# The first half step's output product as seven products of blocks, taken row tile by row tile

## The chip, the cores and the metric

The kernel runs on one core of a Trainium2 chip. The metric is the device time of one execution in microseconds (us). Engines are called as the profile calls them: PE (TensorE, matmul), PEld (its weight loads), DVE (VectorE), ACT (ScalarE), POOL (GpSimd) and SP (SyncE, which issues the DMA transfers).

## The reference

One layer of a diffusion backbone over 1024 latent tokens and 256 context tokens, 1024 features, all in float32. The part that matters here is the first half step and the norm after it:

```python
def swiglu(h, w_in, w_out):
    a, b = jnp.split(h @ w_in, 2, axis=-1)
    return (jax.nn.silu(a) * b) @ w_out
...
    x = x + 0.5 * ml[2] * swiglu(modulate(rms_norm(x, norm1_g), ml[0], ml[1]), ffn1_w_in, ffn1_w_out)
    hx = modulate(rms_norm(x, norm2_g), ml[3], ml[4])
    ... = jnp.split(hx @ w_in, SPLITS, axis=-1)        # token mixers, then a second half step
```

`ffn1_w_out` has 2816 rows (hidden features) and 1024 columns. The modulations `ml` are products of `silu(c)` with `w_mod`.

## The kernel before

Activations lie with the features in partitions: a feature tile is 128 partitions by 512 tokens. The 1024 latents are two chunks, `C0` and `C1`, of 512 tokens. Every matmul operand is split into two parts of fewer bits, `hi` and `lo` (`split`: a cast on ACT, then a subtraction `src - hi` on DVE), and a product is three matmuls: hi x hi, hi x lo, lo x hi.

A scheduler orders each engine's instructions ahead of time; all of a kernel's instructions carry the line number of one helper in the profile, so groups are told apart by the names of the tiles. Tiles come from pools with a fixed number of buffers: `raw` (loaded weights, 3), `wh` and `wl` (split operands, 4 each), a pool of 38 tiles of 4 KB a partition, a pool of 11 smaller ones, and PSUM with 5 banks for products (`ps`), 2 for transposes (`pt`) and 1 more (`po`).

The input products of both half steps and of the token mixers are made by the class `Winograd`: seven products of 2 x 2 blocks instead of eight. Its left operands are column tiles of the weights, summed on POOL (tiles `s`), its right operands (tiles `r`) sums of blocks of the normalised activations. The hidden features of the first half step are stored to a DRAM tensor `hd`, the latents to `xd`.

The output product of the first half step is made in the plain way. For each chunk, all 22 hidden tiles are loaded from `hd` and split (tiles `hid`); then, for groups of three, three and two feature tiles `d`, PE goes through the 22 hidden tiles in three blocks of 8, 8 and 6, with weights loaded and split by `load_w` (tiles `wh`, `wl`). Each `d` has one PSUM bank. When a group is done, DVE adds `gate * ps` to `x` and the result is stored to `xd`:

```python
for ch in (C0, C1):
    ...
    for ds in ((0, 1, 2), (3, 4, 5), (6, 7)):
        ps = {d: ps_s() for d in ds}
        for j0, j1 in ((0, 8), (8, 16), (16, NH)):
            for d in ds:
                wh, wl = load_w(...)
                for j in range(j0, j1):
                    matmul(ps[d], w, hs[j][:, 0], ...)
                    matmul(ps[d], w, hs[j][:, 1], ...)
                    matmul(ps[d], v, hs[j][:, 0], ...)
```

Other work is traced between these products. `steps` are the remaining modulations (`later_mod`: tiles `rawm` are loaded, multiplied by a column of `silu(c)` and added into `macc` on DVE). While the products of `C1` run, the second norm of `C0` is made (`norm0`: squares, a sum over partitions on PE, a reciprocal root, a broadcast by transposes, then the scaled tiles and their splits). `square` sums the squares of `C1` as its feature tiles become ready. After the stage `mix.start` makes ten products of `C0` (the first two of five pairs) while `norm1` makes the right operands of `C1`, whose scaled tiles are `h`, their differences `nt`.

Of the kernel before, what the change touches and what calls it, by code (L numbers as in the profile page):

```python
# [18 lines left out]
P = 128  # L19
D = 1024  # L20
# [29 lines left out]
def tile_dit_layer(  # L50
# [29 lines left out]
    class Engine:  # L80
        """An engine whose instructions stay in the order of the trace while strict[0] is set."""
# [72 lines left out]
    # Vectors over features become columns: one row of 128 each, transposed on the chip.  # L154
# [71 lines left out]
    def rsqrt_cols(a, n):  # L226
        """a ** -0.5 for a [P, n] > 0."""
# [12 lines left out]
    def rstd_cols(accs, n, dim):  # L240
        """(sum over accs and partitions + dim * eps) ** -0.5, tokens in partitions: [P, n / P]."""
# [12 lines left out]
    def bcast(y, n):  # L254
        """Columns y over tokens in partitions, as rows in all partitions: PSUM [P, n]."""
# [5 lines left out]
    def later_mod(m, halves=(0, 1), streams=None):  # L261
        """Columns of modulation m for the latents (0) and, where it is used, the context (1), in steps."""
# [54 lines left out]
    def first_mod(m, half, raws):  # L317
        """Half of modulation m of both streams, on the tensor engine alone; in steps: 6 tiles, 2, the columns."""
# [15 lines left out]
    def second_mod(m, half, raws):  # L334
        """The same of the latents alone; in steps: the products of each tile, their parts, their sums, the columns."""
# [23 lines left out]
    def norm_gain(name, m, gname):  # L359
        """g * (1 + scale) * sqrt(D) by stream; the shift is modulation m."""  # L360
# [59 lines left out]
    def modulated_norm(xs, hh, hl, ch, gain, mod, m):  # L420
        """In steps, for other work to be traced between: squares, sums, two halves of the rest."""
# [20 lines left out]
    def run(steps, n=None):  # L442
        """The next n steps (all without n)."""
# [7 lines left out]
    def out_pieces(w, js, spare=False):  # L451
        """Rows of w_out of hidden tiles js, by halves of the columns."""
# [10 lines left out]
    class Winograd:  # L463
        """Products with normalised latents by Winograd's seven products of 2 x 2 blocks.

        Blocks of the weights: two tiles of columns (a, b) by halves of the input features; blocks of
        the activations: halves of the features by halves of the tokens (C0, C1).
        """

        def __init__(self, xs, gain, mod, m, pairs, plain=False, ahead=3, side_from=None):  # L470
            """pairs: columns of each a and b; plain: with all parts of the latents themselves.

            ahead pairs are begun while the second tokens are normalised. side_from: from this pair on
            the plain left operands are given to side(i, operand) too, as 1, 2 (of a), 0, 4 (of b); those of
            the pairs before come after them.
            """
# [3 lines left out]
            self.n_ahead, self.side, self.started, self.n_left = ahead, None, [], 0  # L480
            self.source, self.ready = self.lefts(pairs, side_from), []

        def keep(self, i, k, src, lo_eng=None):
            """Feature tile k of right operand i."""
# [14 lines left out]
        def norm0(self, in_place=False):  # L499
            """In steps: squares, sums, two halves of the rest."""  # L500
# [13 lines left out]
        def square(self, d):  # L514
            """Feature tile d of the second tokens, squared, into the sums."""
            if d == 0:
                self.acc = [ttile("sq_acc")]
            sq = self.acc[0] if d == 0 else ttile("sq")
            act.activation(out=sq, in_=self.xs(d, C1), func=AF.Square)
            if d == KD - 1:  # L520
                self.acc.append(sq)
            elif d:
                dve.tensor_add(out=self.acc[0], in0=self.acc[0], in1=sq)

# [35 lines left out]
        def part_second(self, k):  # L560
            """The parts of tile k of the second tokens, in the place of the values."""
# [5 lines left out]
        def parts(self, k, ch):  # L567
            """Feature tile k of the latents, its two parts."""
# [3 lines left out]
        def lefts(self, pairs, side_from):  # L572
            """Left operands, in the order they are used."""
# [73 lines left out]
        def first(self):  # L647
            """The products with the first tokens alone: what the rest needs, and a of these tokens."""
# [5 lines left out]
        def start(self, norm):  # L654
            """The first products of some pairs, while the second tokens are normalised."""
# [17 lines left out]
        def start_together(self):  # L673
            """The same in steps: P1 of pairs 0, 1; of 2, 3; of each other; then the second products likewise."""
# [33 lines left out]
        def fetch(self):  # L708
            """What was begun of the next pair and put aside."""
# [14 lines left out]
        def second(self, u):  # L724
            """b of the first tokens."""
# [8 lines left out]
        def third(self, u, v):  # L734
            """a and b of the second tokens."""
# [65 lines left out]
    def turn_tokens(ch, toks, engines=("dve", "act")):  # L801
        """In steps of one feature tile."""
# [26 lines left out]
    def squares(ch, turn):  # L829
        """Squares of the feature tiles as they are turned, added up."""  # L830
# [105 lines left out]
    # Input products of the first half step, and the whole of it for the context.  # L936
# [33 lines left out]
    def context_out(j):  # L970
        """Output products of hidden tiles j - 1 and j for the context."""
# [46 lines left out]
    # Output products for the latents, all hidden tiles of 512 tokens at a time; the second norm starts  # L1018
    # while those of the second tokens are made.
# [9 lines left out]
    for ch in (C0, C1):  # L1029
        o = ch[1]  # L1030
        hs = []
        for j in range(NH):
            hs.append(load_parts("hid", hd[j, :, o : o + 512]))
        for k in range(KD):
            sp.dma_start(out=xs(k, ch), in_=xd[k, :, o : o + 512])
        n_done = 0
        for ds in ((0, 1, 2), (3, 4, 5), (6, 7)):
            ps = {d: ps_s() for d in ds}
            for j0, j1 in ((0, 8), (8, 16), (16, NH)):
                for d in ds:  # L1040
                    wh, wl = load_w(
                        ffn1_w_out[0][j0 * P : j1 * P, d * P : (d + 1) * P].rearrange("(k p) n -> p k n", p=P),
                        (j1 - j0, P),
                    )
                    for j in range(j0, j1):
                        w, v = wh[:, j - j0], wl[:, j - j0]
                        matmul(ps[d], w, hs[j][:, 0], start=j == 0, stop=False)
                        matmul(ps[d], w, hs[j][:, 1], start=False, stop=False)
                        matmul(ps[d], v, hs[j][:, 0], start=False, stop=j == NH - 1)
                    n_done += 1  # L1050
                    if ch == C0:
                        run(steps, 4)
                    elif n_done == 1:
                        run(steps)
                        gain2.update(norm_gain("gain2", 3, "g2"))
                        mix.gain = gain2["l"]
                    elif n_done in (2, 4, 6, 8):
                        run(norms2, 1)
            for d in ds:
                dve.scalar_tensor_tensor(  # L1060
                    out=xs(d, ch), in0=ps[d], scalar=gate1["l"][:, d : d + 1], in1=xs(d, ch),
                    op0=ALU.mult, op1=ALU.add,
                )
                sp.dma_start(out=xd[d, :, o : o + 512], in_=xs(d, ch))
# [4 lines left out]
    # Gated short convolution, and the gates.  # L1069
# [459 lines left out]
```

## Time and profile before

| | |
|---|---|
| median of three runs | 2813.86 us (2812.37 to 2816.64) |
| span of the profiled execution | 2813.7 us |
| busy: PE, PEld, DVE, ACT, POOL | 97%, 81%, 70%, 39%, 19% |
| share of the chain that ended last, by engine | PE 83%, DVE 9%, DMA 3% |

The profiled execution is told by its span, from the first to the last instruction; its time is within 0.2 us of the median of the runs. A busy share is a mean over stages with different limits, so a change in one stage is read in a stretch of the timeline. In a group of instructions, the name before `<-` is the tile written and those after it are the tiles read; what stands after the bar is the busy time, the mean duration of one in ns, the idle time before them and what ended it. In a timeline, an entry has its start, its time in us, its engine and the tiles; `x12` stands for twelve in a row.

### The profile page before, as it was taken

How to read it: one execution, taken by the hardware profiler on the slowest of the kernel's cores; microseconds unless marked ns; L12 is line 12 of the kernel's file. 1: busy time of each engine (PE TensorE's matmuls, PEld its weight loads, DVE VectorE, ACT ScalarE, POOL GpSimd, SP SyncE). 2: the span in 40 equal slices, each digit the busy share in tenths (PEclk: the TensorE clock that was granted, in tenths of full speed). 3: DMA queues.
4: the chain of work that ended last, by engine and by line, in shares of the span. 5: the costliest groups of instructions: out<-in, count | busy, mean ns of one | idle time of the engine just before them, and what ended most of it. 6: DMA issues, size and time to landing. Idle time of an engine off the chain costs nothing.

```text
span 2813.7 us, 37012 instructions
## 1 busy us (share of the span) xinstructions
PE 2725.5 (97%) x13741; PEld 2286.0 (81%) x13741; DVE 1957.2 (70%) x3218; ACT 1096.5 (39%) x2176; POOL 542.3 (19%) x433
## 2 busy tenths in 40 slices
PE   7898999999999989999999999999998999999998
PEld 4687988888888868888999888887886788888887
DVE  5886688877864387676568377776458766666667
ACT  3524333333433243333345167764245222232225
POOL 2541122121001054323123000000014221212111
PEclk8899999999999989999999999999999999999999
DMA  8264433445974333323313300002532311221111
GB/s 303 97 199 151 145 111 126 130 142 158 309 236 130 104 119 106 105 69 97 105 46 122 111 23 5 12 1 90 170 93 90 111 41 51 60 60 53 46 53 68
DMA packets 346910, 298.77 MB, mean 106 GB/s; under 512 B 25430, under 2 KB 276456, under 8 KB 346728
## 3 DMA queue, kind: packets, MB, share of 16 engines
q1 hardware_dynamic: 346728, 296.40, 32.9%
q8 instruction: 108, 1.77, 0.3%
q14 instruction: 74, 0.61, 0.1%
HBM read 247.54 MB, written 48.76 MB: 105 GB/s over the span
## 4 chain that ended last, share of the span: by engine, by line
PE 83%; DVE 9%; DMA 3%; issue 2%; ACT 2%; SPq 0%; POOL 0%; ACTq 0%; DVEq 0%; POOLq 0%
PE ps L88 73%; PE po L88 6%; PE pt L88 4%; DVE wl L88 2%; DVE r L88 1%; DVE nt L88 1%; DVE macc L88 1%; DMA raw<-in_ffn_w_out_dram 1%; DMA rawm<-in_w_mod_dram 1%; DVE wo L88 1%; DMA hid<-hd 1%; DVE h L88 1%; DVE uc L88 0%; SPq L88 0%; DMA mcol<-mrow 0%
## 5 line engine op out<-in xcount | busy, mean ns | idle before, releaser
L88 PE MATMUL ps<-r,wl 128*128 128x512 f32 x5280 | 1242.0, 394 | 36.9 <-ACT wl L88 12.8
L88 PEld LDWEIGHTS ps<-r,wl 128*128 128x128 f32 x5280 | 995.5, 190 | 256.1 <-ACT wl L88 16.4
L88 ACT CAST wl<-s 128x512 fp32r<-128x512 f32 x256 | 158.6, 620 | 330.3 <-PE ps L88 274.5
L88 ACT CAST wl<-raw 128x512 fp32r<-128x512 f32 x230 | 142.3, 620 | 245.7 <-PE ps L88 165.8
L88 DVE TENSOR_TENSOR wl<-raw,wl 128x512 fp32r<-128x512 f32 x228 | 167.1, 733 | 99.9 <-ACT wl L88 98.8
L88 DVE TENSOR_TENSOR wl<-s,wl 128x512 fp32r<-128x512 f32 x256 | 217.4, 850 | 11.6 <-ACT wl L88 9.8
L88 POOL TENSOR_TENSOR s<-raw,s 128x512 f32<-128x512 f32 x64 | 99.1, 1549 | 624.2 <-DVE wl L88 618.9
L88 PE MATMUL ps<-hid,wh 128*128 128x512 f32 x704 | 217.2, 390 | 1.4 <-ACT wh L88 1.4
L88 ACT CAST wh<-raw 128x1024 fp32r<-128x1024 f32 (+2 forms) x100 | 97.9, 982 | 251.5 <-PE ps L88 208.6
L88 DVE SCALAR_TENSOR_TENSOR x<-ps,gate_l,x 128x512 f32<-128x512 f32 (+1 forms) x200 | 140.7, 726 | 79.1 <-PE ps L88 78.8
L88 POOL TENSOR_TENSOR sq_acc<-sq_acc,sq 128x512 f32<-128x512 f32 (+1 forms) x33 | 41.8, 1268 | 765.4 <-ACT sq L88 764.6
L88 POOL TENSOR_TENSOR s<-raw 128x512 f32<-128x512 f32 x64 | 91.2, 1424 | 399.4 <-DMA raw<-in_ffn_w_in_dram 164.5
L88 DVE TENSOR_TENSOR wl<-raw,wh 128x1024 fp32r<-128x1024 f32 (+1 forms) x92 | 109.6, 1192 | 67.5 <-ACT wh L88 65.8
L88 PEld LDWEIGHTS ps<-hid,wh 128*128 128x128 f32 x704 | 131.7, 188 | 30.2 <-ACT wh L88 2.6
L88 DVE SCALAR_TENSOR_TENSOR macc<-rawm,silu_c,macc 128x512 f32<-128x512 f32 x168 | 141.4, 859 | 12.0 <-DMA rawm<-in_w_mod_dram 11.0
L88 PE MATMUL ps<-hid,wo 128*128 128x512 f32 (+1 forms) x552 | 147.7, 381 | 0.4 <-DVE x L88 0.3
L88 DVE TENSOR_TENSOR u<-u,ps 128x512 f32<-128x512 f32 x168 | 114.3, 680 | 46.6 <-PE ps L88 46.3
L88 PE MATMUL ps<-wh,r 128*128 128x256 f32 x768 | 141.5, 285 | 0.0
L88 PE MATMUL ps<-gh,wo 128*128 128x512 f32 (+1 forms) x368 | 135.5, 380 | 1.5 <-ACT wo L88 1.5
L88 PE MATMUL ps<-hid,wl 128*128 128x512 f32 x352 | 136.5, 389 | 0.0
L88 DVE TENSOR_REDUCE m<-ps 128x1 f32<-128x512 f32 (+1 forms) x192 | 112.7, 595 | 20.9 <-PE ps L88 19.8
L88 DVE TENSOR_TENSOR pts<-pt,pts 128x512 fp32r<-128x512 f32 x160 | 108.7, 683 | 18.8 <-ACT pts L88 18.4
(259 smaller groups left out, 4897.1 us busy)
## 6 DMA issues: line engine op xcount, KB each, us to landing
raw<-in_ffn_w_in_dram SPq DMA_DIRECT2D x114, 512.0 KB, 3.7
raw<-in_ffn_w_out_dram SPq DMA_DIRECT2D x76, 512.0 KB, 4.6
rawm<-in_w_mod_dram SPq DMA_DIRECT2D x128, 256.0 KB, 4.1
raw<-in_w_in_dram SPq DMA_DIRECT2D x57, 512.0 KB, 4.0
hid<-hd SPq DMA_DIRECT2D x44, 256.0 KB, 6.2
rawm<-in_w_mod_dram SPq DMA_DIRECT2D x16, 512.0 KB, 8.1
xd<-x SPq DMA_DIRECT2D x32, 256.0 KB, 8.6
x<-xd SPq DMA_DIRECT2D x32, 256.0 KB, 6.1
```

What stands on the lines that cost most here:

```text
L88: inst = getattr(self.engine, name)(*args, **kw)
```

## The change

The output product is made as seven products of blocks too. Its left operands are blocks of the weights (halves of the 2816 rows by halves of the 1024 columns), its right operands blocks of the hidden features (halves of the hidden features by `C0` and `C1`). Both chunks' hidden features are loaded whole, 512 KB at a time, and stay unsplit in 22 tiles. Each of the seven products goes through its 11 row tiles; a row tile needs one left and one right operand, each split into a `wl` or a `wh` tile, and feeds four column tiles in four PSUM banks. The sums of blocks are made on POOL, in place of the hidden tiles for the right operands, and in six tiles `ws` for the left ones. The products run in the order 1, 2, 5, 6, 7, 4, 3; after each, DVE folds its four banks into `chain` (tiles `u`) or into `x`.

```diff
+    def row_products(w, nk, raws, add, after=lambda i, k: None):
+        ...
+        def lefts(i):
+            for k in range(nk):
+                if i in (1, 2, 4, 3, 6):
+                    if k % 2 == 0:
+                        t, n = raw_tile(), min(2, nk - k)
+                        rows(t[:, :n], k, i in (2, 4, 3), i != 4, n)
+                    src = t[:, k % 2]
+                if i == 5:
+                    ...
+                    pool.tensor_add(out=s, in0=t[:, 0], in1=t[:, 1])
+                elif i in (6, 3):
+                    ...
+                    if i == 6:
+                        pool.tensor_sub(out=s, in0=s, in1=src)
+                    else:
+                        pool.tensor_sub(out=s, in0=src, in1=s)
+                elif i == 7:
+                    t = raw_tile()
+                    load(t[:], w[k * P : (k + 1) * P, :].rearrange("p (a n) -> p a n", a=2))
+                    pool.tensor_sub(out=t[:, 0], in0=t[:, 0], in1=t[:, 1])
+                    src = t[:, 0]
+                yield src
+        def right(i, k):
+            (b11, b12), (b21, b22) = ((t[:, 0], t[:, 1]) for t in (raws[k], raws[nk + k]))
+            if i == 5:
+                pool.tensor_sub(out=b11, in0=b12, in1=b11)
+            elif i == 6:
+                pool.tensor_sub(out=b11, in0=b22, in1=b11)
+            elif i == 7:
+                pool.tensor_sub(out=b12, in0=b22, in1=b12)
+            elif i == 4:
+                pool.tensor_sub(out=b11, in0=b11, in1=b21)
+            return {2: b21, 7: b12, 3: b22}.get(i, b11)
+        ...
+        for i in (1, 2, 5, 6, 7, 4, 3):
+            ps = [ps_s() for _ in range(4)]
+            for k, left in enumerate(lefts(i)):
+                l, r = parts(left, "wl"), parts(right(i, k), "wh")
+                for d in range(4):
+                    wh, wl = (l[:, v, d * P : (d + 1) * P] for v in range(2))
+                    matmul(ps[d], wh, r[:, 0], start=k == 0, stop=False)
+                    matmul(ps[d], wh, r[:, 1], start=False, stop=False)
+                    matmul(ps[d], wl, r[:, 0], start=False, stop=k == nk - 1)
+                after(i, k)
+            for d in range(4):
+                if i == 1:
+                    chain[d] = ttile("u")
+                    act.copy(out=chain[d], in_=ps[d])
+                elif i == 2:
+                    c = ttile("c")
+                    dve.tensor_add(out=c, in0=chain[d], in1=ps[d])
+                    add(d, C0, c)
+                elif i == 5:
+                    add(d, C1, ps[d])
+                    add(d + 4, C1, ps[d])
+                elif i == 6:
+                    dve.tensor_add(out=chain[d], in0=chain[d], in1=ps[d])
+                    add(d, C1, chain[d])
+                ...
+                else:
+                    add(d, C1, ps[d])
+            after(i, nk)
...
-    for ch in (C0, C1):
-        ...
+    hs = []
+    for j in range(NH):
+        hs.append(atile("hid", (P, 2, 512)))
+        load(hs[j][:].rearrange("p a b -> p (a b)"), hd[j])
+    for k in range(KD):
+        for ch in (C0, C1):
+            sp.dma_start(out=xs(k, ch), in_=xd[k, :, ch[1] : ch[1] + 512])
+    def add1(d, ch, t):
+        dve.scalar_tensor_tensor(
+            out=xs(d, ch), in0=t, scalar=gate1["l"][:, d : d + 1], in1=xs(d, ch), op0=ALU.mult, op1=ALU.add
+        )
+    def after1(i, k):
+        ...
+        if i in (2, 5, 6) and k < NH // 2:
+            run(steps, 2)
+        if (i, k) == (7, 0):
+            run(steps)
+            gain2.update(norm_gain("gain2", 3, "g2"))
+            mix.gain = gain2["l"]
+        ...
+        if i == 3 and k in (1, 3, 5, 7):
+            run(norms2, 1)
+    row_products(ffn1_w_out[0], NH // 2, hs, add1, after1)
```

`square` is called in the order in which the feature tiles of `C1` become ready (4 to 7 after product 7, 0 to 3 after product 3), and counts its calls in place of looking at `d`. The remaining lines of the diff are comments and descriptions that were taken out.

More of the change, by code (lines that the diff above doesn't have):

```diff
@@ L480, in __init__ @@
             self.n_ahead, self.side, self.started, self.n_left = ahead, None, [], 0
+            self.n_squares = 0
             self.source, self.ready = self.lefts(pairs, side_from), []
@@ L786, in ffn, with rows, raw_tile, parts @@
                             after(ch, dt)
+    def row_products(w, nk, raws, add, after=lambda i, k: None):
+        R = P * nk
+        def rows(t, k, lower, left, n=1):
+            o, c = k * P + R * lower, 512 * (not left)
+            load(t, w[o : o + n * P, c : c + 512].rearrange("(a p) n -> p a n", p=P))
+        def raw_tile():
+            return wpool.tile([P, 2, 512], F32, tag="raw", name=uniq("raw"), bufs=3)
+        sums = {}
+        def lefts(i):
[7 more added lines that the diff above has]
+                    t = raw_tile()
+                    rows(t[:, :1], k, False, False)
+                    rows(t[:, 1:], k, True, False)
+                    if k % 2 == 0:
+                        sums[k] = atile("ws", (P, 2, 512))
+                    s = sums[k - k % 2][:, k % 2]
+                    pool.tensor_add(out=s, in0=t[:, 0], in1=t[:, 1])
+                    src = s
+                elif i in (6, 3):
+                    s = sums[k - k % 2][:, k % 2]
+                    if i == 6:
+                        pool.tensor_sub(out=s, in0=s, in1=src)
+                    else:
+                        pool.tensor_sub(out=s, in0=src, in1=s)
+                    src = s
+                elif i == 7:
+                    t = raw_tile()
+                    load(t[:], w[k * P : (k + 1) * P, :].rearrange("p (a n) -> p a n", a=2))
[13 more added lines that the diff above has]
+            return {2: b21, 7: b12, 3: b22}.get(i, b11)
+        def parts(src, tag):
+            t = wpool.tile([P, 2, 512], F32R, tag=tag, name=uniq(tag), bufs=W_BUFS)
+            split(src, t[:, 0], t[:, 1])
+            return t
+        chain = {}
+        for i in (1, 2, 5, 6, 7, 4, 3):
[22 more added lines that the diff above has]
+                    add(d, C1, chain[d])
+                elif i == 7:
+                    dve.tensor_add(out=chain[d], in0=chain[d], in1=ps[d])
+                    add(d + 4, C1, chain[d])
+                elif i == 4:
+                    dve.tensor_sub(out=chain[d], in0=chain[d], in1=ps[d])
+                    add(d + 4, C0, chain[d])
+                else:
+                    add(d, C1, ps[d])
+            after(i, nk)
@@ L1028, in tile_dit_layer @@
     norms2, norm1, gain2 = mix.norm0(in_place=True), mix.norm1(), {}
-    for ch in (C0, C1):
[L1030 to L1058, printed above, removed]
-            for d in ds:
[L1060 to L1064, printed above, removed]
@@ new lines, in tile_dit_layer, with done @@
+    hs = []
[10 more added lines that the diff above has]
+    def after1(i, k):
+        def done(ds, ch):
+            for d in ds:
+                sp.dma_start(out=xd[d, :, ch[1] : ch[1] + 512], in_=xs(d, ch))
@@ L1065, in tile_dit_layer @@
                 if ch == C1:
                     mix.square(d)
+        if i in (2, 5, 6) and k < NH // 2:
[4 more added lines that the diff above has]
+            mix.gain = gain2["l"]
+        if k == NH // 2:
+            if i == 2:
+                done(range(4), C0)
+            elif i == 7:
+                done(range(4, KD), C1)
+            elif i == 4:
+                done(range(4, KD), C0)
+            elif i == 3:
+                done(range(4), C1)
```

9 lines of the change are left out of this document (5 added, 4 removed).

## The prediction

> **What bounds the kernel now.** I read the cores' spans first, then the table of stretches, then the groups by shape inside the stretch that the change replaces, then the timeline of DVE and POOL where both are busy.
>
> ```profile
> core 0: 2813.7 us, clock 0.984
> ```
>
> ```profile
> PE 2725.5 (97%) x13741; PEld 2286.0 (81%) x13741; DVE 1957.2 (70%) x3218; ACT 1096.5 (39%) x2176; POOL 542.3 (19%) x433
> ```
>
> The span of this one execution is 2813.7 us and the median of the three runs 2813.86 us: 0.2 us lie around it, and I add changes to the median. PE is busy for 97% of it. From the table of stretches (start:end, length, then busy time and count for each engine, granted clock, DMA share, GB/s):
>
> ```profile
> 724.30:969.30 245.00, 243.59 (x1079) 199.97 (x1077) 131.50 (x175) 83.43 (x112) 12.64 (x7) 1.00 0.62 197
> 724.00:754.00 30.00, 30.00 (x135) 24.45 (x134) 24.63 (x36) 12.88 (x19) 0.00 (x0) 1.00 1.03 356
> 969.30:1033.30 64.00, 51.72 (x206) 38.72 (x204) 50.74 (x69) 31.51 (x58) 30.17 (x21) 0.89 0.29 95
> 1000.00:1008.00 8.00, 2.58 (x5) 1.47 (x6) 8.00 (x8) 4.41 (x8) 6.77 (x5) 0.62 0.16 66
> 1064.00:1300.00 236.00, 236.00 (x1043) 195.46 (x1042) 165.56 (x245) 74.92 (x127) 79.20 (x57) 1.00 0.30 96
> ```
>
> The output products of the first half step are the first row: 245 us, PE idle for 1.4 us, POOL almost unused (7 instructions). 1079 matmuls in 245 us are 0.227 us each. So this stage is bound by PE alone, and DVE has 113 us to spare in it. After it come 64 us with 12 us of PE gaps, while the second norm is made.
>
> **The part taken away.** The two chunks make 2 x 8 x 22 x 3 = 1056 matmuls of 128x512. Seven products of 11 row tiles, 4 column tiles and 3 terms make 924. 132 fewer at 0.227 are 30 us: if PE stays fed the stage takes 215 us, 30.7 a product and 2.7 a row tile.
>
> **What feeds it.** Groups by shape inside 724 to 969:
>
> ```profile
> L88 DVE TENSOR_TENSOR wl<-raw,wh 128x1024 fp32r<-128x1024 f32 x32 | 40.1, 1256 | 21.1 <-ACT wh L88 20.5 <-PE pt L88 0.3
> L88 DVE SCALAR_TENSOR_TENSOR macc<-rawm,silu_c,macc 128x512 f32<-128x512 f32 x28 | 21.0, 749 | 2.8 <-DMA rawm<-in_w_mod_dram 2.3
> L88 DVE TENSOR_TENSOR hid<-hid 128x512 fp32r<-128x512 f32 x23 | 15.3, 692 | 12.4 <-ACT hid L88 12.3
> L88 ACT CAST hid<-hid 128x512 fp32r<-128x512 f32 x23 | 14.3, 621 | 19.2 <-DMA hid<-hd 18.8
> L88 DVE SCALAR_TENSOR_TENSOR x<-ps,gate_l,x 128x512 f32<-128x512 f32 x15 | 11.2, 747 | 13.1 <-PE ps L88 13.1
> L88 DVE SCALAR_TENSOR_TENSOR cx<-cacc,gate_c,cx 128x256 f32<-128x256 f32 x8 | 3.2, 476 | 0.0
> ```
>
> A row tile of a product is fed by two splits (one left, one right): two ACT casts of 0.62 and two DVE subtractions of 0.69. That is 1.24 us on ACT and 1.4 on DVE in 2.7 us, so either engine alone would keep up. New are 88 POOL instructions of 128x512, the sums of blocks: products 5 and 6 have two a row tile, 7 has two, 4 and 3 have one. POOL's own time is not the trouble either. Six rows of its timeline, the first four with DVE busy on tiles in SBUF, the last two without:
>
> ```profile
> 999.56 1.72 POOL L88 TENSOR_TENSOR s<-s,raw 128x512 f32<-128x512 f32 x1
> 1001.25 1.72 POOL L88 TENSOR_TENSOR s<-raw,raw 128x512 f32<-128x512 f32 x1
> 1002.92 1.74 POOL L88 TENSOR_TENSOR r<-nt,r 128x512 fp32r<-128x512 f32 x1
> 1004.62 1.71 POOL L88 TENSOR_TENSOR nt<-h,x 128x512 f32<-128x512 f32 x1
> ...
> 1027.90 1.29 POOL L88 TENSOR_TENSOR s<-s,raw 128x512 f32<-128x512 f32 x1
> 1029.15 1.29 POOL L88 TENSOR_TENSOR s<-raw,raw 128x512 f32<-128x512 f32 x1
> ```
>
> And DVE in the microseconds of the first four:
>
> ```profile
> 997.52 1.27 DVE L88 TENSOR_TENSOR h<-x,pt 128x512 f32<-128x512 f32 x2
> 998.71 1.45 DVE L88 TENSOR_TENSOR nt<-h,nt 128x512 f32<-128x512 f32 x1
> 1000.08 1.75 DVE L88 TENSOR_TENSOR r<-h,r 128x512 fp32r<-128x512 f32 x1
> 1001.75 1.75 DVE L88 TENSOR_TENSOR r<-nt,r 128x512 fp32r<-128x512 f32 x1
> 1003.43 0.67 DVE L88 TENSOR_TENSOR uc<-uc,ps 128x512 f32<-128x512 f32 x1
> ```
>
> Here is the price that decides. A DVE instruction with both inputs in SBUF and a POOL instruction do not run side by side: they take turns, one of each per 1.68 us (starts at 1000.08, 1001.75, 1003.43; POOL at 999.56, 1001.25, 1002.92). Of that 0.60 is DVE's (two in 1.19 from 997.52 to 998.71) and 1.08 POOL's. One that reads PSUM is not held: 0.67 at 1003.43, inside POOL's 1.74. The splits of the new stage all have both inputs in SBUF.
>
> Demand on that shared turn, with the counts from the changed program's instruction order (the first splits are done before PE begins): 147 splits x 0.60 = 88; 28 macc steps x 0.66 (0.749 against 0.692 for a split) = 18; 16 adds to x from a chain tile x 0.66 = 11; 11 square and macc sums x 0.60 = 7; 8 cx x 0.40 = 3; POOL 88 + 3 square sums = 91 x 1.08 = 98. Together 225 us, against 215 for PE. The POOL order puts all 22 right operands of products 5 and 7 into product 1, and those of 6 and 4 one product early. By product, in the order of execution:
> - product 1: 15 splits 9.0, 7 macc 4.6, 22 POOL 23.8: 37;
> - product 2: 22 splits 13.2, 7 macc 4.6, 2 sums 1.2, cx 3.2, 3 POOL 3.2: 25;
> - product 5: 13.2, 4 adds 2.6, 7 macc 4.6, 1 sum 0.6, 16 POOL 17.3: 38;
> - product 6: 13.2, 7 macc 4.6, 1 sum 0.6, 20 POOL 21.6: 40;
> - product 7: 13.2, 4 adds 2.6, 16 POOL 17.3: 33;
> - product 4: 13.2, 4 adds 2.6, 4 sums 2.4, 4 POOL 4.3: 23;
> - product 3: 13.2, 4 adds 2.6, 3 sums 1.8, 10 POOL 10.8: 28.
>
> Where that is below 30.7, PE sets the time: 37 + 31 + 38 + 40 + 33 + 31 + 31 = 241. Beside this DVE has 24 evictions that read PSUM, at 0.6 to 0.67 each; they are not held by POOL and fit into its turns, so they cost nothing where POOL runs; elsewhere DVE has time. ACT gets 154 casts of 0.62 where before it had 44 of these and 48 longer ones, and no row shows it held by POOL.
>
> A rule on this price: the Trainium skill (SBUF — State Buffer, section "SBUF: two separate sides") says that the pair of ports shared by the two engines is an exclusive lock, held for the whole instruction, taken by a DVE instruction with two SBUF inputs when POOL reads SBUF. By whole instructions the sum of turns would be 263 us (rival 5). The trace agrees that neither engine gets on while the other runs, but shows a pair in 1.68 us, not in 1.98.
>
> **Boundaries.** Four of the five banks are taken by a product, so the next one gets its second bank only after an eviction. The changed order has DVE reach the evictions after two row tiles of the next product, where four are buffered; it then waits for PE (13.1/15 = 0.9 us each in the x row above) and does four evictions (2.4 us), and only then the next split. Products 2, 4 and 3 have spare turns to catch up; into 5, 6 and 7 I charge one row tile each, 2.7 x 3 = 8 us. The ends are 0 (the buffers hide it) and 6 x 3.3 = 20. It lies nearest to the x row's waits, hence 8. The stage: 249 us, **4 more than the 245 of before**.
>
> **What comes after it.** Before, the norm of the first 512 tokens ran under the second chunk's products; now that chunk is complete only after product 4, and the norm sits in product 3. PE order after the stage, before the change:
>
> ```profile
> 969.30 2.88 PE L88 MATMUL ps<-r,wl 128*128 128x512 f32 x12
> 983.60 0.60 PE L88 MATMUL pt<-ident,rs_y 128*128 128x128 f32 x4
> 983.95 15.01 PE L88 MATMUL ps<-r,wl 128*128 128x512 f32 x65
> 1002.79 1.68 PE L88 MATMUL ps<-r,wl 128*128 128x512 f32 x3 [3.83 <-ACT wl L88]
> ```
>
> The broadcast that starts the second norm's DVE work (983.60) stands after 55 products (12 + 12 + 31); in the changed order after 83. 28 x 0.227 = 6 us later, with the same 120 products to cover it, and the cover already ended at 1002.79. So +6 us. The ends are 0 and the whole 14 us from 969.3 to 983.6. The first right tiles of the mixers (r of the first tokens) now stand behind the last evictions in DVE's queue; two row tiles of product are ahead of them, so I add nothing.
>
> **SyncE's queue.** 44 loads of 256 KB become 22 of 512 KB, and both chunks' x are loaded at once, 16 x 256 KB ahead of product 2's weights.
>
> ```profile
> hid<-hd SPq DMA_DIRECT2D x44, 256.0 KB, 6.2
> ```
>
> That is 5.8 + 2.1 = 7.9 MB earlier; at the 356 GB/s of the second stretch 22 us. Product 2's weights are wanted 37 us after the start, so it is covered; with a fed PE, 31 us. I add nothing; if the cover fails, up to 10 us. The other rows (4 gain instructions, stores of x in another order, the remaining modulation steps, spread over products 2, 5, 6) change no count.
>
> Sum: 2814 + 4 + 6 = **2824 us**.
>
> **Rivals.**
> 1. *PE stays fed (faster).* The four-deep buffers absorb the collisions, because half of POOL's work is not urgent. For it: in 1064 to 1300 PE has no gap with 57 POOL instructions. Against: that is 57 in 236 us, here 91 in 225. It decides when the lag stays under four row tiles (10.9 us): stage 215, 2814 - 30 + 6 = 2790. Chance 0.13.
> 2. *Turns are packed perfectly.* No loss at boundaries and idle turns of products 2 and 4 used: 228. 2814 - 17 + 6 = 2803. Chance 0.12.
> 3. *The clock falls too.* Between 1000 and 1008 PE had gaps and the granted clock was 0.62. If the gaps of products 1, 5, 6, 7 bring the mean to 0.89 as in the third stretch, their 148 us take 1/0.89, 18 more: 2842. Chance 0.13. The Trainium skill (TensorE: Matmul & The Clock Gate, "Part 1: The HAM clock gate") has the clock halved after an idle window of about 3.4 us; by that rule gaps of 1 us a row tile leave it alone, and the 3.83 us gap that ended at 1002.79, beside the 0.62, fits it.
> 4. *The start is late for its loads.* The 10 us above: 2834. Chance 0.09.
>
> 5. *Each turn lasts a whole instruction.* If a pair took 1.29 + 0.69, the turns would be 91 x 1.29 + 127 x 0.69/0.60 = 263 instead of 225, the stage 249 + 38 = 287: 2862. The pairs in 1.68 us speak against it. Chance 0.03.
>
> My forecast has 0.5. That the matmuls are not fewer is excluded by the count.
>
> **How the numbers follow.** Range: 2798 to 2842, from between rivals 1 and 2 up to rival 3; it leaves out rival 1, rival 5 and half of what lies at rival 3 (0.13 + 0.03 + 0.05). A difference of 0.2% (5.6 us) is about what a measurement can tell from none. Faster: rivals 1 and 2 less a little, 0.22. Same: the lower part of the forecast, with boundaries near 0 (2816 to 2819), 0.18. Slower: the rest, 0.60.
>
> **What would show it.** Right: in the new stage the subtractions wl and wh average about 1.0 us instead of 0.69, POOL's sums 1.5 or more; PE's gaps end on DVE wl or wh in products 1, 5, 6; products 2 and 4 take 31 us. The broadcast comes about 20 us after the stage. Wrong: PE without gaps at 0.227 a matmul (rival 1), gaps ended by DMA raw (rival 4), or a granted clock under 0.9 in the stage (rival 3).

## The result and the profile after

| | before | after |
|---|---|---|
| median | 2813.84 us (2812.37 to 2816.64) | 2837.05 us (2836.12 to 2840.54) |
| span of the profiled execution | 2813.7 us | 2835.9 us |
| ratio to before, 95% interval | | 1.008 (1.0066 to 1.0094) |

The change makes the kernel 23.2 us slower. 10 were forecast. First the page's line of busy times, then the group of the stage's products in the whole span:

```profile
PE 2710.2 (96%) x13609; PEld 2264.4 (80%) x13609; DVE 2070.3 (73%) x3308; ACT 1112.2 (39%) x2242; POOL 680.2 (24%) x521
L88 PE MATMUL ps<-wh,wl 128*128 128x512 f32 x924 | 227.5, 405 | 28.1 <-DVE wh L88 18.3
```

132 matmuls are gone, PE is busy for 15.3 us less, and still the end comes later: the products alone have 28.1 us of waits ahead of them. The table of stretches of after; first the stage as a whole, then the products 1, 2, 5, 6, 7, 4, 3 in their order, divided by the count of their 132 matmuls each, then what follows (start:end, length, busy time and count of PE, PEld, DVE, ACT and POOL, granted clock, DMA share, GB/s):

```profile
725.30:987.20 261.90, 229.91 (x946) 179.91 (x945) 242.07 (x272) 102.33 (x184) 144.42 (x91) 0.95 0.53 174
...
725.30:761.70 36.40, 32.52 (x134) 25.44 (x132) 34.37 (x26) 10.14 (x18) 33.15 (x22) 0.95 0.86 307
761.70:800.27 38.57, 32.12 (x135) 26.19 (x136) 30.90 (x45) 17.99 (x33) 8.61 (x7) 0.91 0.63 207
800.27:852.52 52.25, 36.68 (x137) 26.64 (x136) 52.18 (x43) 14.29 (x26) 46.52 (x29) 0.91 0.59 186
852.52:890.34 37.82, 34.41 (x136) 25.38 (x134) 37.75 (x42) 12.59 (x23) 22.99 (x15) 0.94 0.27 87
890.34:920.80 30.46, 30.43 (x133) 24.63 (x132) 28.19 (x35) 12.27 (x22) 12.07 (x8) 1.00 0.58 179
920.80:950.83 30.03, 30.03 (x134) 24.70 (x133) 26.71 (x34) 16.77 (x30) 11.12 (x8) 1.00 0.50 165
950.83:987.20 36.37, 33.72 (x145) 26.94 (x144) 31.97 (x53) 18.29 (x32) 9.97 (x7) 0.95 0.25 80
987.20:1064.80 77.60, 60.22 (x236) 45.46 (x235) 66.14 (x88) 38.32 (x70) 39.32 (x27) 0.85 0.34 112
```

The stage takes 261.9 us where the plain products took 245.0. DVE is busy for 242.07 of them (131.50 before) and POOL for 144.42. In the third product (5 in the numbering) DVE is busy for 52.18 of 52.25 us, and POOL got through 29 sums there. The groups by shape in the stage show why DVE is so busy:

```profile
L88 DVE TENSOR_TENSOR wh<-hid,wh 128x512 fp32r<-128x512 f32 x75 | 81.7, 1093 | 1.7 <-ACT wh L88 1.7
L88 POOL TENSOR_TENSOR hid<-hid,hid 128x512 f32<-128x512 f32 x33 | 54.6, 1660 | 20.0 <-DVE wh L88 20.0
L88 DVE TENSOR_TENSOR wl<-ws,wl 128x512 fp32r<-128x512 f32 x33 | 41.6, 1260 | 3.4 <-ACT wl L88 3.2
L88 DVE TENSOR_TENSOR wl<-raw,wl 128x512 fp32r<-128x512 f32 x42 | 38.1, 913 | 11.2 <-ACT wl L88 10.5
L88 DVE SCALAR_TENSOR_TENSOR macc<-rawm,silu_c,macc 128x512 f32<-128x512 f32 x28 | 29.9, 1068 | 1.5 <-DMA rawm<-in_w_mod_dram 1.3
```

150 splits took 161.4 us, 1.08 us each instead of 0.69. POOL's 33 sums of two hidden tiles took 1.66 us each, all 88 sums 1.62 on the mean, instead of 1.29. The largest single gap of PE in the stage is 6.5 us long and ends at 768.15, the start of product 2. PE there, and what stood ahead of it in the timelines of ACT, DVE and POOL:

```profile
768.15 10.02 PE L88 MATMUL ps<-wh,wl 128*128 128x512 f32 x36 [6.49 <-ACT wl L88]
...
763.98 0.62 ACT L88 CAST acch<-macc 128x512 fp32r<-128x512 f32 x1 [11.74 <-DVE macc L88]
764.51 0.61 ACT L88 CAST wh<-hid 128x512 fp32r<-128x512 f32 x1
765.03 2.04 ACT L88 COPY u<-ps 128x512 f32<-128x512 f32 x4
766.93 0.65 ACT L88 CAST wh<-hid 128x512 fp32r<-128x512 f32 x1
767.45 2.20 ACT L88 CAST wl<-raw 128x512 fp32r<-128x512 f32 x4
...
760.50 3.44 DVE L88 SCALAR_TENSOR_TENSOR macc<-rawm,silu_c,macc 128x512 f32<-128x512 f32 x2
...
759.99 3.41 POOL L88 TENSOR_TENSOR hid<-hid,hid 128x512 f32<-128x512 f32 x2
```

ACT stood for 11.74 us at the cast of a modulation sum (`acch<-macc`), while DVE was busy without a break; the last two of that sum's steps, beside POOL's sums for later products, took 3.44 us together (two of them take 1.53 us in run 3). Behind it in ACT's queue stood the four copies of product 1 out of PSUM, and behind these product 2's first weights. The page of the profile never names this as a POOL matter: PE's wait is put down to ACT `wl`.

### The profile page after: what moved, and what is told of

Read it like the earlier page. It is cut to its first block, busy times and chain, and to the rows that moved or that the text cites. A ratio compares the mean times of both kernels' runs of the same rounds, so it can differ in the third digit from the quotient of the medians.

```text
span 2835.9 us, 36998 instructions
## 1 busy us (share of the span) xinstructions
PE 2710.2 (96%) x13609; PEld 2264.4 (80%) x13609; DVE 2070.3 (73%) x3308; ACT 1112.2 (39%) x2242; POOL 680.2 (24%) x521
## 3 DMA queue, kind: packets, MB, share of 16 engines
q8 instruction: 107, 1.75, 0.3%
## 4 chain that ended last, share of the span: by engine, by line
PE 57%; DVE 9%; issue 2%; ACT 2%; DMA 1%; POOL 1%; SPq 0%; DVEq 0%; ACTq 0%; POOLq 0%
PE ps L88 51%; PE po L88 3%; PE pt L88 3%; DVE wl L88 2%; DMA raw<-in_ffn_w_out_dram 1%; DVE r L88 1%; DVE wh L88 1%; DVE x L88 1%; POOL ws L88 1%; DVE nt L88 1%; DVE macc L88 1%; DVE u L88 1%; DVE uc L88 0%; POOL hid L88 0%; DVE y L88 0%
## 5 line engine op out<-in xcount | busy, mean ns | idle before, releaser
L88 ACT CAST wl<-raw 128x512 fp32r<-128x512 f32 x274 | 169.2, 620 | 283.2 <-PE ps L88 175.8
L88 DVE TENSOR_TENSOR wl<-raw,wl 128x512 fp32r<-128x512 f32 x272 | 205.4, 756 | 96.3 <-ACT wl L88 94.4
L88 PE MATMUL ps<-wh,wl 128*128 128x512 f32 x924 | 227.5, 405 | 28.1 <-DVE wh L88 18.3
L88 PEld LDWEIGHTS ps<-wh,wl 128*128 128x128 f32 x924 | 177.8, 195 | 76.5 <-DVE wh L88 26.8
L88 DVE TENSOR_TENSOR u<-u,ps 128x512 f32<-128x512 f32 x180 | 122.3, 681 | 51.2 <-PE ps L88 50.7
L88 DVE SCALAR_TENSOR_TENSOR macc<-rawm,silu_c,macc 128x512 f32<-128x512 f32 x168 | 150.3, 913 | 11.6 <-DMA rawm<-in_w_mod_dram 10.7
L88 DVE TENSOR_TENSOR pts<-pt,pts 128x512 fp32r<-128x512 f32 x160 | 108.9, 683 | 18.7 <-ACT pts L88 18.3
L88 PEld LDWEIGHTS ps<-wh,r 128*128 128x128 f32 x768 | 120.6, 192 | 0.0
L88 PEld LDWEIGHTS ps<-hid,wo 128*128 128x128 f32 x552 | 101.2, 188 | 23.0 <-DVE x L88 3.5
L88 ACT CAST pts<-pt 128x512 fp32r<-128x512 f32 x160 | 93.3, 592 | 64.8 <-PE pt L88 62.4
```

The costliest lines, as they stand in the source:

```text
L88: inst = getattr(self.engine, name)(*args, **kw)
```

## The experiments

The theory in all of them is the prediction's: POOL's sums hold DVE, DVE holds PE. Where the gap at product 2 comes from was open, and later where the last microseconds after the stage go. Each kernel's edit is against the changed kernel unless said otherwise. Each ratio is to the kernel before, run on the same chip.

### 1. No sums

```diff
 # lefts: products 5, 6, 7, 3 use the loaded block itself
-    pool.tensor_add / tensor_sub(...)      # 4 places
 # right: the blocks as they are
-    pool.tensor_sub(out=b11 or b12, ...)   # 4 places
```

> The changed kernel without its 88 block sums: left and right operands are the plain blocks, so the values are not the reference's; loads, splits, matmuls, evictions and modulation steps stay. Theory 1 (turns: POOL and DVE take turns on SBUF, which is what stretched the stage from 215 to 262 us): DVE's own 127 + 24 us no longer collide, PE stays fed, the stage takes 215 to 225 us and the kernel 2790 to 2802. Rival 1 (the row tiles, the four banks and the order of evictions and loads cost the time, whoever sums): the stage stays above 250, the kernel above 2825.

2790.29 us (2785.28 to 2792.07), ratio 0.991 (0.9894 to 0.9927). Its stage, in the same columns:

```profile
727.39:942.30 214.91, 213.20 (x946) 175.32 (x945) 162.75 (x272) 103.66 (x184) 4.15 (x3) 1.00 0.62 211
```

Without the sums the stage takes the 215 us of a PE that is fed, and the kernel the 2790 us of rival 1. So the products, their order, banks and loads are sound, and the whole 46.8 us between this and after hangs on the 88 sums. PE's longest wait in this stage is 1.71 us, at the start of product 2, although the 16 loads of `x` stand ahead of that product's weights in SyncE's queue (SPq) as they do in after:

```profile
739.39 11.36 SPq L88 DMA_DIRECT2D x<-xd  x16
...
759.21 8.48 PE L88 MATMUL ps<-wh,wl 128*128 128x512 f32 x36 [1.71 <-ACT wl L88]
```

### 2. The sums on DVE

```diff
-    pool.tensor_add(...) / pool.tensor_sub(...)
+    dve.tensor_add(...) / dve.tensor_sub(...)    # all 8 places
```

> The same sums, made on DVE instead of POOL. Theory 1: 88 x 0.60 = 53 us of DVE replace 91 x 1.08 = 98 us of turns; DVE's whole work in the stage is 127 + 24 + 53 = 204 us, under PE's 215. Stage 215 to 240, kernel 2795 to 2815, that is at least 20 us faster than with POOL. Rival 2 (DVE is simply overloaded: it was busy 249 of 262 us): 53 us more work on it make the stage longer, kernel 2850 or more.

2811.6 us (2809.77 to 2814.33), ratio 0.9994 (0.9984 to 1.0003).

```profile
725.13:961.10 235.97, 220.74 (x946) 177.59 (x945) 213.78 (x360) 103.75 (x184) 5.36 (x3) 0.98 0.56 193
```

DVE now has 360 instructions in the stage instead of 272, and is busy for less time: 213.78 us instead of 242.07 (the 249 of the expectation was too high). Without any sums it was busy for 162.75 us (run 1). So on the mean a sum costs DVE 0.58 us when DVE makes it, and 0.90 us when POOL does. Taking 88 instructions onto the busier engine made the kernel 25 us faster.

### 3. Fills in place of the sums

POOL keeps its 88 instructions, in the same places and on the same tiles, but fills the tiles and reads nothing.

```diff
-    pool.tensor_sub(out=s, in0=s, in1=src)
+    pool.memset(s, 1.0)                          # likewise in all 8 places
```

> The 88 sums are replaced, on POOL and in their places, by a fill of the same 128x512 tile with ones: values are not the reference's; order, waits and buffers stay, but POOL reads nothing. Theory 1, if the turn is taken for POOL's reads: DVE is not held, its splits take 0.69, kernel within 6 us of the one without sums. Rival 4 (POOL itself is too slow or too late in the chain sum, cast, subtract): its instructions are still there in the chain, kernel above 2815. If fills hold DVE as sums do, splits stay above 0.9 us and the kernel above 2815 too, which the splits' duration tells apart from rival 4.

2792.28 us (2789.66 to 2796.34), ratio 0.9921 (0.9904 to 0.9938). Stage, and the groups of two kinds of split and of two of the fills:

```profile
723.03:938.30 215.27, 213.56 (x947) 175.21 (x946) 163.04 (x272) 103.89 (x184) 43.05 (x78) 1.00 0.61 211
...
L88 DVE TENSOR_TENSOR wh<-hid,wh 128x512 fp32r<-128x512 f32 x75 | 51.3, 684 | 8.2 <-ACT wh L88 8.1
L88 DVE TENSOR_TENSOR wl<-ws,wl 128x512 fp32r<-128x512 f32 x33 | 23.4, 710 | 10.9 <-ACT wl L88 10.8
L88 POOL MEMSET ws<- 128x512 f32 x33 | 16.8, 529 | 58.9 <-DVE wl L88 58.6
L88 POOL MEMSET hid<- 128x512 f32 x31 | 16.6, 535 | 21.0 <-DVE wh L88 19.8
```

The chain of waits through POOL is still there, and the time is within 2 us of the kernel without sums. The splits are back at 0.68 and 0.71 us. A fill is also shorter than a sum, 0.53 us, so the totals alone do not part "reads" from "occupies". The timeline does. Here a fill lies wholly inside a split, and the split takes its 0.68 us, where a sum that takes turns adds 1.08 us to one:

```profile
781.55 0.68 DVE L88 TENSOR_TENSOR wh<-hid,wh 128x512 fp32r<-128x512 f32 x1
781.69 0.53 POOL L88 MEMSET ws<- 128x512 f32 x1 [0.96 <-DVE wl L88]
```

The Trainium skill (SBUF — State Buffer, section "Who interferes with whom") says that a DVE instruction with two SBUF inputs contends with a GpSimd instruction that reads SBUF and not with one that only writes it. The trace agrees: 684 ns beside fills, 1093 beside sums.

### 4. Half of the sums on DVE

```diff
-    pool. ...  in lefts (44 sums)
+    dve. ...
```

> The 44 sums of left blocks on DVE, the 44 of right blocks on POOL. Theory (POOL's reads hold DVE, in proportion to their number): about half of the way from 2837 to the 2812 of all sums on DVE, 2820 to 2828, and the gap at the start of product 2 stays, because the right operands run in product 1. Rival: what hurts is that a left sum on POOL is late for its own split; then all of the gain is there, 2810 to 2815.

2826.27 us (2823.98 to 2827.73), ratio 1.0043 (1.0026 to 1.006). Halfway between 2837.05 and 2811.6 is 2824.3. So the price follows the number of POOL's sums, and not the lateness of the left ones (the other half alone, right sums on DVE, was not run). The gap at product 2 stays (6.54 us), since the right operands made early are still POOL's.

### 5. The modulation steps of the stage moved into the mixers

```diff
-        if i in (2, 5, 6) and k < NH // 2:
-            run(steps, 2)
         if (i, k) == (7, 0):
-            run(steps)
 ...
+        run(steps, 9)          # in each of the 8 passes of the mixers
```

> The changed kernel with the remaining modulation steps (28 macc steps and what belongs to them) moved out of the stage into the mixers' loop, nine steps a pass; sums stay on POOL. Theory 1: 28 x 0.66 = 18 us of turns leave the stage, and the 6.5 us gap ahead of product 2, where ACT stood behind the cast of macc, goes: stage 235 to 247, kernel 2812 to 2825 if the mixers take the steps free. Rival 3 (that gap comes from product 2's loads, behind 16 loads of x in SyncE's queue): the gap stays, and the kernel is above 2828.

2827.96 us (2825.44 to 2832.49), ratio 1.005 (1.0031 to 1.007): 9 us better than after, between the two accounts, and the gap at product 2 stayed. That was a misreading of the edit: the steps which hold the gap were begun in the stage before, and their cast `acch` still stood in ACT's queue with an idle time of 11.76 us. The stage fell to 244 us, 18 less than after; half of that was lost again behind it. Run 7, which has the steps at the same place, shows where.

### 6. The modulation sum cast earlier

One step fewer per hidden tile in the stage before moves that cast from the end of product 1 to its start.

```diff
-STEPS = (0, 6, 6, 6, 7, 7, 8, 8, 8, 15)
+STEPS = (0, 6, 6, 6, 7, 7, 8, 8, 8, 14)
```

> One step fewer of the modulation work per hidden tile in the stage before, so that the modulation sum which in the changed kernel is cast at the end of product 1 is cast near its beginning, and no cast of macc stands in ACT's queue ahead of product 2's first casts. Everything else as in the changed kernel. Theory: the 6.5 us gap at the start of product 2 is ACT waiting in order for that sum, whose DVE steps POOL's sums hold; the gap falls under 2 us and the time to 2829 to 2833. Rival: the gap is the turns themselves (POOL runs 22 right operands in product 1) or late loads: the gap, or several small ones of the same sum, stay, 2835 to 2839.

2838.72 us (2835.95 to 2842.13), ratio 1.0089 (1.0074 to 1.0104): no gain. The gap at product 2 shrank to 3.94 us and did not go. ACT's timeline ahead of it:

```profile
762.76 1.14 ACT L88 CAST wl<-raw 128x512 fp32r<-128x512 f32 x2 [3.33 <-DMA raw<-in_ffn_w_out_dram]
```

With the cast out of the way ACT waits for the weights of product 2 themselves. They stand behind the 16 loads of `x` in SyncE's queue (run 9 moves these), and in this kernel behind four loads of `cx` as well: they are issued from 755.61 on, in after from 751.90. My theory had only the cast. Another gap came in its place: at product 5's start PE waited 6.24 us, because DVE stood 3.25 us at a modulation step whose load had not landed, and the two splits after it took 1.74 and 1.75 us:

```profile
801.36 0.61 DVE L88 TENSOR_SCALAR macc<-rawm,silu_c 128x512 f32<-128x512 f32 x1 [3.25 <-DMA rawm<-in_w_mod_dram]
```

### 7. Sums on DVE, modulation later and cast earlier

Runs 2 and 6 together, and the steps of run 5, 12 a pass.

```diff
-STEPS = (..., 15)
+STEPS = (..., 14)
-        run(steps, 9)
+        run(steps, 12)         # against runs 2 and 5 together
```

> All sums on DVE, the remaining modulation steps in the mixers (12 a pass), and one step fewer per hidden tile in the stage before. Theory: turns are gone and DVE has 28 steps less in the stage; stage 220 to 226 us, no gap over 3 us in it, 2797 to 2804. Rival: DVE alone is too slow at the boundaries: 2808 to 2813 as with the sums on DVE alone.

2822.42 us (2819.88 to 2824.33), ratio 1.0031 (1.0019 to 1.0042): missed by both accounts. The stage has the length that the theory said, 225 us, though one gap of 4.13 us stayed in it, at product 2; the mixers lost the gain. Windows of this kernel (the stage, then 55 us at the mixers' start), of run 2 (55 us of the mixers), and one line of this kernel's DVE:

```profile
723.53:948.60 225.07, 214.13 (x926) 173.90 (x925) 192.10 (x318) 98.75 (x175) 5.18 (x3) 0.98 0.51 175
1030.00:1085.00 55.00, 42.18 (x160) 33.01 (x160) 43.57 (x74) 14.82 (x25) 17.39 (x13) 0.82 0.48 156
```

```profile
1040.00:1095.00 55.00, 54.98 (x245) 44.92 (x244) 52.65 (x80) 19.70 (x33) 25.78 (x17) 1.00 0.45 146
```

```profile
1071.40 0.16 DVE L88 TENSOR_TENSOR modl<-mcol,bcol 128x4 f32<-128x4 f32 x1 [8.29 <-DMA mcol<-mrow]
```

160 matmuls against 245 in 55 us: 85 x 0.225 = 19 us lost. A DVE addition of 0.16 us waited 8.29 us for a modulation's columns to come back through a DMA, and all of DVE's work for the products waited behind it. The clock fell to 0.82 with the gaps.

### 8. More products as cover for the second norm

```diff
-RESIDENT, AH2, AH3 = 2, 5, 6
+RESIDENT, AH2, AH3 = 2, 7, 6     # on run 7
```

> The kernel before this one in the list, with 7 instead of 5 pairs begun with the first tokens before the second norm's operands are needed (48 more products, 10.9 us, as cover). Theory: the 8.2 and 4.0 us gaps after the stage are the second norm coming late, and cover fills them: 8 to 11 us faster than the kernel without it, 2788 to 2795. Rival: the gaps are ACT and DVE busy with the norm and late with the weights' splits, which more pairs need too: within 3 us of the kernel without it, or slower.

2814.49 us (2812.34 to 2817.51), ratio 1.0001 (0.9992 to 1.0011): 7.9 us better than run 7, just under the 8 to 11 of the theory. But the gaps that it was to fill did not shrink: in place of one of 8.21 and one of 3.97 us there is one of 17.67. Runs 10 and 11 read it without the moved steps.

### 9. The loads of x spread out

On run 2, the 16 loads of `x` no longer stand together ahead of product 2's weights.

```diff
-    for k in range(KD):
-        for ch in (C0, C1):
-            sp.dma_start(out=xs(k, ch), in_=xd[...])
 ...
+        if (i, k) == (1, 9):
+            x_load(range(4), C0)
+        elif (i, k) == (2, 4):
+            x_load(range(KD), C1)
+        elif (i, k) == (6, 4):
+            x_load(range(4, KD), C0)
```

> All sums on DVE (2811.6), and the 16 loads of x no longer all at the start of the stage: 4 in product 1's tenth row tile, 8 in product 2, 4 in product 6. Theory: with the sums off POOL the gap at product 2's start (5.2 us there) is the weights of product 2 landing behind 4.2 MB of x; it falls under 2 us and the time to 2806 to 2809. Rival: ACT's order sets it (the cast of the modulation sum stands ahead): the gap stays over 4 us, 2810 to 2813.

2808.24 us (2806.83 to 2812.0), ratio 0.9982 (0.9973 to 0.9991). ACT at the same place in run 2, where PE's gap is 5.21 us, and then in this kernel, where it is 1.20:

```profile
757.31 0.62 ACT L88 CAST acch<-macc 128x512 fp32r<-128x512 f32 x1 [1.42 <-DMA cx<-cxd]
757.84 2.04 ACT L88 COPY u<-ps 128x512 f32<-128x512 f32 x4
759.75 2.21 ACT L88 CAST wl<-raw 128x512 fp32r<-128x512 f32 x4
```

```profile
754.41 0.62 ACT L88 CAST wh<-hid 128x512 fp32r<-128x512 f32 x1 [1.06 <-PE ps L88]
754.94 1.13 ACT L88 CAST wl<-raw 128x512 fp32r<-128x512 f32 x2
758.32 0.62 ACT L88 CAST acch<-macc 128x512 fp32r<-128x512 f32 x1 [2.25 <-DVE macc L88]
758.85 2.04 ACT L88 COPY u<-ps 128x512 f32<-128x512 f32 x4
```

With the weights ahead of most of `x` in SyncE's queue, their casts also stand ahead of the modulation's cast and of the four copies in ACT's order. In run 2 ACT comes to the weights only behind those, and no wait for their load is recorded. So this run moved two things at once, the load and ACT's order. That the scheduler makes the order to fit the load would join them into one cause; it is my reading and is not shown.

### 10 and 11. Run 9 with 6 and with 7 pairs ahead

> The kernel before with 6 instead of 5 pairs begun before the second norm's operands (24 products more as cover, 5.4 us). Theory: the second norm lacks cover; 4 to 6 us faster than the kernel before. Rival: DVE and ACT are the limit in the norm, since each further pair also needs its weights split ahead of the norm's own work: within 2 us of the kernel before.

> The same with 7 pairs (48 products more, 10.9 us). Theory: 8 to 11 us faster than with 5 pairs, as the change from 5 to 7 gave 8 with the modulation steps moved. Rival: that gain came only from gaps that the moved steps had made in the mixers; here within 3 us of the kernel with 5 pairs.

2803.86 us (2799.0 to 2804.65), ratio 0.9962 (0.9949 to 0.9974), and 2802.39 us (2799.12 to 2806.56), ratio 0.996 (0.9947 to 0.9972). The first of two more pairs gives 4.4 us, the second 1.5, with intervals that overlap. PE alone by 50 us in run 9 and in run 11, at the end of the stage and after it (length, busy time and count of PE, granted clock, DMA share, GB/s):

```profile
950.00:1000.00 50.00, 39.29 (x171) 0.91 0.32 106
1000.00:1050.00 50.00, 42.44 (x158) 0.89 0.36 116
```

```profile
950.00:1000.00 50.00, 47.58 (x211) 0.97 0.40 127
1000.00:1050.00 50.00, 33.07 (x138) 0.83 0.33 110
```

Run 11 makes 40 products more in the first 50 us and 20 fewer in the next: half of the cover is given back, since the gaps of 8.20 and 3.97 us become one of 17.64. That the weights of the further pairs are split ahead of the norm's own work would explain this; it was not tried.

### 12. The kernel before, with 7 pairs

> The kernel before the change, with 7 instead of 5 pairs begun before the second norm's operands. Theory: the cover lacks there too (gaps of 3.8 and 2.6 us), but less than after the change, where the broadcast comes later: 2 to 6 us faster, 2808 to 2812. Rival: before the change the cover was enough: within 2 us of it or slower. Either way the rest of the 11 us of the best version is what the seven products bring.

2807.73 us (2805.63 to 2811.5), ratio 0.9979 (0.997 to 0.9988). The cover is worth 7.2 us without the change, more than the 2 to 6 expected, where run 11 had 5.8 from it. So of the 11 us by which run 11 beats the kernel before, half or more has nothing to do with the seven products. These (with sums on DVE and `x` later) leave 5.3 us between runs 11 and 12, which were not made on the same chip, and the two intervals just overlap, at 0.997.

## Why the prediction was right or wrong

**Right: the sign and the mechanism.** The forecast was 2824, in 2798 to 2842; it came to 2837.05. The splits average 1.08 us ("about 1.0"), POOL's sums 1.62 ("1.5 or more"), and 18.3 of the 28.1 us that the products wait end on DVE `wh`. Run 1 measured the fed stage: 214.91 us where the step said 215, and 2790.29 where rival 1 said 2790. Rivals 2 and 5 are out, since the stage took neither 228 nor 287 us. (The 1.98 us of rival 5 adds two durations. Undisturbed, instructions of these two kinds start 1.25 us and 0.60 us apart, in the rows at 1027.90 and 1029.15 and at 997.52, so even a full wait would have been nearer to 1.85.)

**The sum, term by term.** Start of the stage 1.0 us later (725.3 for 724.3); the stage +16.9 where +4 stood; after it +4.3 where +6 stood. Together that is the 22.2 us between the two profiled executions; the medians differ by 23.2.

**The tail was nearly right.** PE's order after the stage, in after:

```profile
1009.53 0.60 PE L88 MATMUL pt<-ident,rs_y 128*128 128x128 f32 x4
...
1026.74 1.22 PE L88 MATMUL ps<-r,wl 128*128 128x512 f32 x2 [8.20 <-ACT wl L88]
1031.94 1.65 PE L88 MATMUL ps<-r,wl 128*128 128x512 f32 x3 [3.97 <-DVE wl L88]
```

The broadcast comes 22.3 us after the stage (14.3 before; "about 20" was said). The first gap grew from 3.83 to 8.20 us. The next one, before it 2.64 us at 1007.53, is 3.97: together 5.7 us more. The rest of the kernel wins 1.4 us of that back.

**The step that failed is the stage's size: 249 forecast, 262 measured.** By product, in their order, forecast and measured: 37 and 36.4; 31 and 38.6; 38 + 40 + 33 and the 8 of the boundaries, 119, and 52.2 + 37.8 + 30.5 = 120.5; 31 and 30.0; 31 and 36.4. 7.6 of the 13 us are product 2 and 5.4 the last one, product 3. In both I let PE set the time and put the waits at nothing.

**Product 2.** The turns had 25 us of demand there, less than PE's 31. But PE waited 6.5 us at its start, and the clock was 0.91 in it: PE was busy for 32.12 us with 135 matmuls, which at 0.227 are 30.6, 1.5 us less. Two things that I had looked at bear on the wait:
- "The remaining modulation steps ... change no count". They change none, but the cast of their sum stands in ACT's queue ahead of product 2's weights, and POOL's sums held up DVE, which makes that sum. In after this is the wait that the trace shows (11.74 us of ACT).
- "SyncE's queue", where 7.9 MB at 356 GB/s came to 22 us and were called covered. I had taken the bytes and not their place in the queue. In after no wait of ACT for these weights is recorded, and runs 1 and 3, with the same loads at the same place, have a gap of 1.71 us there. So the loads do not make the gap by themselves; they are the next thing in line, as run 6 shows (3.33 us of ACT). Run 9 took the gap from 5.2 to 1.2 us by moving them, but ACT's order changed with them. Rival 4 ("the start is late for its loads") is not shown for after.

How the 6.5 us in after would divide if the cast alone or the loads alone were out of the way is not known: run 6 changed the order of SyncE's queue too, and the kernel after with only the loads of `x` moved was not run.

**Product 3.** "Products 2, 4 and 3 have spare turns to catch up" held for product 4 alone. At the start of product 3 the casts of its operands stand in ACT's queue behind squares of `x`, which waited for DVE's updates of `x`; the last of three such waits, of 3.41, 2.31 and 2.27 us, and PE's own:

```profile
961.47 0.63 ACT L88 ACTIVATE sq<-x 128x512 f32<-128x512 f32 x1 [2.27 <-DVE x L88]
...
964.45 1.20 PE L88 MATMUL ps<-wh,wl 128*128 128x512 f32 x4 [2.31 <-ACT wh L88]
```

PE waited 2.65 us in this product, the clock was 0.95, and twelve short matmuls of the norm are in it. Without the sums (run 1) there is no such gap.

**The middle was right in part by luck.** POOL ran ahead and did 29 sums in product 5 where 16 were counted, so the three products are right in sum and not one by one. And DVE stood still for only 2.4 of the 120.5 us, so the 8 us charged at the boundaries were not seen as waits. What filled them is near 7.2 us of DVE instructions that the count had left out, small ones and those with one input (last section).

**Rival 3, the clock,** did not set in as stated. Products 1, 5, 6 and 7 had 0.95, 0.91, 0.94 and 1.00, not 0.89 on the mean; product 2, where I had not looked for it, 0.91. In product 5 DVE sets the time, being busy for all but 0.07 us, and a slower PE costs nothing there; in product 2 it is the 1.5 us above. The rule that the prediction names with this rival would leave the clock alone in gaps this short, and product 5 does not bear that out: its longest gap is 2.67 us. In the whole stage PE was busy for 229.91 us with 946 matmuls, where run 1 has 213.20 with as many; how much of the 16.7 us set the time, outside product 2, was not separated.

## What to carry to other kernels

Before elementwise work goes to an idle POOL, count what DVE does meanwhile on tiles in SBUF: here each such sum cost DVE more (0.90 us) than making the sum itself (0.58), and the 88 sums were cheaper on the engine that was already the busier one. Work that is not urgent is not harmless either: an eager queue, a modulation's cast or an early block of loads can hold up whatever stands behind it in order. When a stage is compressed, recheck each "covered" load and each piece of cover after it at the new, shorter times.

## What was not expected of the hardware

A small DVE instruction is held by POOL as long as a large one. Three lines of DVE in product 5, under POOL's sums:

```profile
825.60 1.51 DVE L88 TENSOR_SCALAR macc<-rawm,silu_c 128x512 f32<-128x512 f32 x1
...
828.72 1.24 DVE L88 TENSOR_TENSOR modl<-mcol,bcol 128x4 f32<-128x4 f32 x1
829.99 1.22 DVE L88 TENSOR_SCALAR gain_l<-modl 128x8 f32<-128x8 f32 x1
```

An addition of four columns took 1.24 us; in run 7, without POOL's sums beside it, the same took 0.16. That is 1.08 us more, as much as for an instruction of 128x512. And `TENSOR_SCALAR`, with one tensor in SBUF as input, was held too: 1.51 us, against 0.48 for the same instruction (a group of four) in the kernel with fills. The prediction had counted instructions with two inputs alone, and none of the small ones.
